# RWKV chunk inverse: the identity taken into each masked factor, the add replaced by a copy on ScalarE

## The chip, the cores and the metric

The kernel runs on one core of a Trainium2 chip. The metric is the device time of one execution in microseconds. Before the change it is 2451.85 us, the median of three runs (2451.59 to 2456.05).

## The reference

Two model blocks follow one another on a sequence of 256 tokens of width 1024, in fp32. The first block is a SwiGLU feed-forward layer, a mixing layer and a second feed-forward layer. The mixing layer has two parts side by side: dilated window attention, and a bidirectional RWKV-7 recurrence. The second block has two layers of windowed attention with an mLSTM, a dense feed-forward layer and a mixture of eight experts. The change touches the RWKV part alone. Per direction and head, the reference walks over the tokens with a 64 x 64 state:

```
def _rwkv7_step(state, inp):
    r, w, k, v, kk, kka = inp
    sa = jnp.einsum('dbhvk,dbhk->dbhv', state, kk)
    state = state * w[..., None, :] - sa[..., :, None] * kka[..., None, :] + v[..., :, None] * k[..., None, :]
    y = jnp.einsum('dbhvk,dbhk->dbhv', state, r)
    return state, y
```

There are 8 heads of 64 and 2 directions. The kernel doesn't walk token by token. It cuts the 256 tokens into four chunks of 64. Inside a chunk the removal terms (sa) depend on one another through a strictly triangular 64 x 64 matrix, so a chunk needs the inverse of "identity minus a strictly triangular matrix".

## The kernel before

`program` (L1634) runs the layers one after another. Each is written as a Python generator that yields now and then, and helpers such as `weave` run two of them in turn. `mix1` (L778) runs the RWKV part with `weave(self.rwkv(mp, me, R, yT), side, 4)`: after every fourth yield of `rwkv`, one step of `side` is emitted; what is left of `side` is emitted after it. `side` is `mod(0)` (L829). It streams 24 MB of modulation weights in 24 loads of 1 MB through three buffers, multiplies each load by a conditioning vector in four products of 512 columns (L837), and after every second load copies (L840), transposes (L843) and reduces (L845) the outcome. It has 36 steps.

The order of instructions on an engine isn't the order in which they are written. The framework's planner takes, engine by engine, what it believes to be ready, in the order of writing, by its own estimate of durations; each engine then runs its list in order, waiting on semaphores.

`rwkv` (L508) works on 8 groups: 4 pairs of heads (`ct`), each in 2 directions (`d`). `group(ct, d, sh)` (L539) prepares decays and scaled keys on ScalarE, VectorE and GpSimd (L569 to L608, the first products being L569 and L570), multiplies them (L623), and masks the outcome into `LM` (L626). A group holds four units `u`, each two chunks in two partition halves of 64 lanes (`halves`), so every small product below is 64 x 64 and the two halves use different parts of TensorE. After each direction pair comes `finish(ct)`. PSUM buffers have the tags c0, c1, c2, two buffers each; a group uses the tag of its number modulo 3.

The inverse is built by doubling the size of the blocks that are inverted (1 to 64 in six levels). `X` is the inverse so far, `Y` its transpose. Level 0 has no product: GpSimd masks `LM` (L654, once per half), VectorE adds the identity (L656) and transposes (L657). Each of the levels 1 to 5 has a product with `LM` into PSUM (L663, 8 small products), a mask on VectorE that reads PSUM (L665), a product with `Y` (L670, again 8), an add on VectorE that reads PSUM (L672), and a 32 x 32 block transpose on VectorE (L673); the last level adds into `Y` (L675) and has no transpose. A level ends with a yield. After the levels the inverse is multiplied with the right-hand sides (L680, 8 products of 128 columns), copied (L682, L684), and used to the end of the group (L715).

In fp32 each product is two TensorE instructions in the profile, so a line with 8 products shows 16.

Of the kernel before, what the change touches and what calls it, by code (L numbers as in the profile page):

```python
# [13 lines left out]
OP = mybir.AluOpType  # L14
# [8 lines left out]
FT = 22  # L23
# [10 lines left out]
class Builder:  # L34
# [473 lines left out]
    def rwkv(self, mp, me, R, yT):  # L508

        nc = self.nc  # L510
# [6 lines left out]
        lvl = self.load_const(mp, "k_lvl", nc.sync)  # L517
# [16 lines left out]
        def tmpt(name, bufs=1):  # L534
            return me.tile([128, S], F32, name=name, bufs=bufs)

        halves = [slice(0, 64), slice(64, 128)]

        def group(ct, d, sh):  # L539
            tag = "c%d" % ((2 * ct + d) % DEEP)  # L540
# [76 lines left out]
            LM = me.tile([128, 4, 4, 64], F32, name="LM", bufs=DEEP)  # L617
# [18 lines left out]
            if d == 1:  # L636
                s = tmpt("ksum")
# [5 lines left out]
            lv = self.psum(4, 64, tag=tag)  # L643
# [4 lines left out]
            nc.scalar.copy(RHS[:, :, 64:128], lv)  # L648
            square = lambda n, bufs=1: mp.tile([128, 4, 64], F32, name=n, tag=n + tag, bufs=bufs)
            over = lambda i: lvl[:, i][:, None, :].to_broadcast([128, 4, 64])  # L650
            X, Y = square("X"), square("Y")

            for c in range(2):
                nc.gpsimd.tensor_tensor(Y[halves[c]], LM[halves[c], :, 2 * c],  # L654
                                        lvl[halves[c], 0][:, None, :].to_broadcast([64, 4, 64]), op=OP.mult)
            nc.vector.tensor_tensor(Y, Y, over(6), op=OP.add)  # L656
            nc.vector.transpose(X, Y)  # L657
            for li in range(1, 6):
                fp = self.psum(4, 64, tag=tag)
                for u in range(4):  # L660
                    for c in range(2):
                        ps = halves[c]
                        nc.tensor.matmul(fp[ps, u], LM[ps, u, 2 * c], X[ps, u], start=True, stop=True)  # L663
                F = square("FT")
                nc.vector.tensor_tensor(F, fp, over(li), op=OP.mult)  # L665
                yp = self.psum(4, 64, tag=tag)
                l, r_ = (Y, F) if li < 5 else (F, Y)
                for u in range(4):
                    for ps in halves:
                        nc.tensor.matmul(yp[ps, u], l[ps, u], r_[ps, u], start=True, stop=True)  # L670
                if li < 5:
                    nc.vector.tensor_tensor(X, yp, X, op=OP.add)  # L672
                    nc.vector.transpose(Y, X)  # L673
                else:
                    nc.vector.tensor_tensor(Y, yp, Y, op=OP.add)  # L675
                yield
            pp = self.psum(4, 128, tag=tag)
            for u in range(4):
# [9 lines left out]
            for u in range(4):  # L688
                t, hh = divmod(u, 2)
# [5 lines left out]
            yp = self.psum(2, 2, 64, tag=tag)  # L695
            for u in range(4):
                t, hh = divmod(u, 2)
# [7 lines left out]
            for u in range(4):  # L705
                t, hh = divmod(u, 2)
# [66 lines left out]

        shs = [{} for _ in range(4)]
        g = [group(ct, d, shs[ct]) for ct in range(4) for d in range(2)]
        yield from chain(g[0], g[1], finish(0, shs[0]), g[2], g[3], finish(1, shs[1]), g[4], g[5], finish(2, shs[2]), g[6], g[7], finish(3, shs[3]))

# [806 lines left out]
def host_consts():  # L1584
    f = np.float32
    out = {"k_ident": np.eye(128, dtype=f)}
    i = np.arange(128)
    t, s = i[:, None], i[None, :]
    same = (t // 64) == (s // 64)
    lm = np.zeros((128, 2, 2, 2, 64), f)  # L1590
    lv = np.zeros((128, 7, 64), f)
    for d in range(2):
        before = (t < s) if d == 0 else (t > s)
        incl = before | (t == s)
        b, n = before[:64, :64], incl[:64, :64]
        for c in range(2):
            lm[c * 64:c * 64 + 64, d, c] = np.stack([-b.astype(f), -n.astype(f)], 1)
            lm[64 - c * 64:128 - c * 64, d, c] = np.stack([b, n], 1)
    for li, m in enumerate((1, 2, 4, 8, 16, 32)):
        lv[:, li] = np.tile(((t // (2 * m) == s // (2 * m)) & (t // m != s // m))[:64, :64], (2, 1))  # L1600
    lv[:, 6] = np.tile(np.eye(64), (2, 1))
    out["k_lm"] = lm
    out["k_lvl"] = lv
    out["k_blk"] = same.astype(f)
    q = np.arange(S)
    diff = np.abs(q[:, None] - q[None, :])
    cnt = (diff <= 64).astype(np.int64) + (diff % 4 == 0) + (diff % 16 == 0)
    bias = np.where(cnt > 0, np.log(np.maximum(cnt, 1).astype(np.float64)), -1e30).astype(f)
    out["k_mask1"] = np.ascontiguousarray(bias.reshape(2, 128, S).transpose(1, 0, 2))
    pos = np.arange(S, dtype=f)  # L1610
    inv = (f(10000.0) ** (-np.arange(0, 64, 2, dtype=f) / f(64))).astype(f)
    ang = (pos[:, None] * inv[None, :]).astype(f)
    c, sn = np.cos(ang).astype(f), np.sin(ang).astype(f)
    C = np.concatenate([c, c], 1)
    Sg = np.concatenate([-sn, sn], 1)
    tab = np.stack([C / 8, Sg / 8, C, Sg], 1).astype(f)
    t4 = np.arange(S)
    iq = (f(10000.0) ** (-np.arange(16, dtype=f) / f(16))).astype(f)
    ar = ((t4 // 64).astype(f)[:, None] * iq[None]).astype(f)
    ac = ((t4 % 64).astype(f)[:, None] * iq[None]).astype(f)  # L1620
    cr, sr, cc, sc = (np.cos(ar).astype(f), np.sin(ar).astype(f), np.cos(ac).astype(f), np.sin(ac).astype(f))
    C2 = np.concatenate([cr, cr, cc, cc], 1)
    S2 = np.concatenate([-sr, sr, -sc, sc], 1)
    tab2 = np.stack([C2 / 8, S2 / 8, C2, S2], 1).astype(f)
    out["k_rope2"] = np.ascontiguousarray(tab2.reshape(2, 128, 4, 64).transpose(1, 0, 2, 3))
    ok = np.stack([t <= s, t >= s], 1)
    out["k_tri"] = ok.astype(f)
    out["k_trib"] = np.where(ok, 0.0, -1e30).astype(f)
    out["k_iota"] = np.ascontiguousarray(np.broadcast_to(np.arange(1, 257, dtype=f).reshape(2, 128), (128, 2, 128)))
    out["k_rope1"] = np.ascontiguousarray(tab.reshape(2, 128, 4, 64).transpose(1, 0, 2, 3))  # L1630
    return out
# [32 lines left out]
def arrange(inputs):  # L1664
    out = {}
    for n in _RAW:
        a = np.asarray(inputs[n])
        if n not in _WHOLE:
            a = a.reshape(a.shape[1:])
        if n in ("rwkv_w2", "rwkv_a2"):  # L1670
            a = a.reshape(128, 512)
        if n == "w_router_2":
            a = a.reshape(KT, 128, 8).transpose(1, 0, 2)
        out[n] = np.ascontiguousarray(a)
    out["k_vec"] = pack_vec(vec_list(inputs))
    out.update(host_consts())
    return out
# [16 lines left out]
```

## Time and profile before

| what | value |
|---|---|
| median of three runs | 2451.85 us |
| the profiled execution | 2451.68 us |
| its span, first to last instruction | 2449.9 us |
| TensorE products busy | 2346.6 us (96%) |
| VectorE busy | 1614.4 us (66%) |
| ScalarE busy | 1307.0 us (53%) |
| GpSimd busy | 188.2 us (8%) |

The span is one execution on the chip. Busy times are sums over the whole span; the ends of TensorE products are modelled, so a busy TensorE isn't one at its peak. In the rows, PE is a TensorE product, PEld a weight load, DVE is VectorE, ACT is ScalarE, POOL is GpSimd, L665 is line 665 of the kernel. A form such as 64*64 64x128 f32 is the part of the array that is used (rows*columns) and the output (partitions x elements).

### The profile page before, as it was taken

To read this page: it belongs to the slowest core of one execution; us is meant where nothing else is said; L and a number is where in the kernel's file an instruction comes from. 1 tells how busy PE (TensorE), PEld (TensorE's weight loads), DVE (VectorE), ACT (ScalarE), POOL (GpSimd) and SP (SyncE) were. 2 spreads that over 40 slices of the span, in tenths; PEclk is the share of its full clock that TensorE was granted. 3 is DMA by queue.
4 is the path that set the end of the run, shared out by engine and by line. 5 is a ranking of instruction groups with operands and counts; after the bars stand their busy time and mean duration, and the time that the engine had idled before them with its cause. 6 is when DMAs were issued, how large, how long until landed. Compare 5 with 4: busy or idle time off the path is not lost. (4 is left out here: it accounts for less than half of the span.)

```text
span 2449.9 us, 38791 instructions
## 1 busy us (share of the span) xinstructions
PE 2346.6 (96%) x15592; PEld 1963.8 (80%) x15592; DVE 1614.4 (66%) x2427; ACT 1307.0 (53%) x2038; POOL 188.2 (8%) x248
## 2 busy tenths in 40 slices
PE   7998989979998999999999999989999999999996
PEld 7996866659998767799899886778888887788875
DVE  5555667656547466443333464669989989889897
ACT  5543644345545355433223243567887777777764
POOL 0001112110001000200100110020100110020000
PEclk9999999999999999999999999999999999999998
DMA  8654342275652350232322235469999999999993
GB/s 261 198 187 138 122 162 88 81 237 170 202 173 88 102 172 21 70 118 82 110 93 82 83 113 175 135 237 373 335 352 341 343 345 335 352 339 335 365 343 134
DMA packets 281100, 489.56 MB, mean 200 GB/s; under 512 B 11424, under 2 KB 116896, under 8 KB 280912
## 3 DMA queue, kind: packets, MB, share of 16 engines
q1 hardware_dynamic: 280832, 486.80, 58.2%
q8 instruction: 124, 2.03, 0.3%
q14 instruction: 64, 0.52, 0.1%
q0 software_dynamic: 80, 0.21, 0.0%
HBM read 485.92 MB, written 1.05 MB: 199 GB/s over the span
## 5 line engine op out<-in xcount | busy, mean ns | idle before, releaser
L150 DVE TENSOR_TENSOR wlo<-wraw,whi 128x1024 fp32r<-128x1024 f32 (+1 forms) x830 | 975.5, 1208 | 227.9 <-ACT whi L149 221.9
L149 ACT CAST whi<-wraw 128x1024 fp32r<-128x1024 f32 (+1 forms) x832 | 824.6, 1030 | 257.9 <-PE ps L162 102.2
L161 PE MATMUL gu<-xlo,whi 128*128 128x256 f32 x1408 | 394.4, 280 | 4.0 <-DVE xlo L193 2.4
L160 PE MATMUL gu<-xhi,whi 128*128 128x256 f32 x1408 | 394.6, 281 | 0.8 <-ACT xhi L200 0.8
L162 PE MATMUL gu<-xhi,wlo 128*128 128x256 f32 x1408 | 393.8, 280 | 0.0
L161 PE MATMUL gu<-wlo,X 128*128 128x512 f32 (+1 forms) x768 | 291.2, 379 | 4.4 <-DVE wlo L150 3.4
L162 PE MATMUL gu<-whi,X 128*128 128x512 f32 (+1 forms) x768 | 286.2, 373 | 0.0
L160 PE MATMUL gu<-whi,X 128*128 128x512 f32 (+1 forms) x768 | 285.1, 374 | 0.0
L161 PEld LDWEIGHTS gu<-xlo,whi 128*128 128x128 f32 x1408 | 264.8, 188 | 5.3 <-DVE xlo L193 2.9
L160 PEld LDWEIGHTS gu<-xhi,whi 128*128 128x128 f32 x1408 | 264.7, 188 | 2.2 <-ACT xhi L200 1.4
L162 PEld LDWEIGHTS gu<-xhi,wlo 128*128 128x128 f32 x1408 | 265.2, 188 | 0.0
L161 PEld LDWEIGHTS gu<-wlo,X 128*128 128x128 f32 x768 | 144.7, 188 | 45.5 <-DVE wlo L150 21.3
L160 PEld LDWEIGHTS gu<-whi,X 128*128 128x128 f32 x768 | 144.7, 188 | 25.5
L162 PEld LDWEIGHTS gu<-whi,X 128*128 128x128 f32 x768 | 144.7, 188 | 23.6
L274 DVE TENSOR_TENSOR hh<-sg,gu 128x256 f32<-128x256 f32 x88 | 36.8, 418 | 164.6 <-ACT sg L272 164.6
L161 PE MATMUL acc<-wlo,xhi 128*128 128x512 f32 (+1 forms) x368 | 141.8, 386 | 3.1 <-DVE wlo L150 3.1
L160 PE MATMUL acc<-whi,xhi 128*128 128x512 f32 (+1 forms) x368 | 140.8, 385 | 2.5 <-ACT whi L149 1.1
L162 PE MATMUL acc<-whi,xlo 128*128 128x512 f32 (+1 forms) x368 | 141.6, 385 | 0.1
L161 PE MATMUL dn<-wlo,hT 128*128 128x512 f32 x352 | 140.6, 399 | 0.0
L162 PE MATMUL dn<-whi,hT 128*128 128x512 f32 x352 | 138.6, 394 | 0.0
L160 PE MATMUL ps<-whi,hhi 128*128 128x512 f32 x352 | 137.2, 390 | 0.0
L162 PE MATMUL ps<-whi,hlo 128*128 128x512 f32 x352 | 137.1, 390 | 0.0
(461 smaller groups left out, 3740.7 us busy)
## 6 DMA issues: line engine op xcount, KB each, us to landing
wraw<-in_exp_w_dram SPq DMA_DIRECT2D x235, 1024.0 KB, 7.0
wraw<-in_w_mod_dram SPq DMA_DIRECT2D x48, 1024.0 KB, 5.2
wraw<-in_w_in_dram SPq DMA_DIRECT2D x29, 1024.0 KB, 5.2
wraw<-in_exp_w_dram SPq DMA_DIRECT2D x58, 512.0 KB, 6.7
wraw<-in_ffn_w_dram SPq DMA_DIRECT2D x28, 1024.0 KB, 5.3
wraw<-in_ffn_w_gate_dram SPq DMA_DIRECT2D x20, 1024.0 KB, 5.7
wraw<-in_ffn_w_up_dram SPq DMA_DIRECT2D x20, 1024.0 KB, 5.5
wraw<-in_ffn_w_down_dram SPq DMA_DIRECT2D x16, 1024.0 KB, 5.1
```

The lines of the kernel that those rows point to most:

```text
L149: nc.scalar.copy(hi, raw[:, k0:k0 + n])
L150: eng.tensor_tensor(lo, raw[:, k0:k0 + n], hi.bitcast(F32), op=OP.subtract)
L160: mm(out, l[0], r[0], start=start, stop=False)
L161: mm(out, l[0], r[1], start=False, stop=False)
L162: mm(out, l[1], r[0], start=False, stop=stop)
L274: nc.vector.tensor_tensor(hh, sg, pg[:, 1], op=OP.mult)
```

## The change

Level 0 now goes through the same loop as the others. In every level the product with `LM` is accumulated in PSUM onto an identity, which is put there by one more product per half: the 64 x 64 identity times four copies of itself, 256 columns. The masks now include the diagonal, so the masked factor is "identity plus masked product". The product with `Y` then gives the new `X` (or, in the last level, the new `Y`) without an add, and ScalarE copies it from PSUM. Level 0 multiplies `LM` by the identity and writes its masked product into `X`. `X` and `Y` become new tiles in each level, in the same one buffer each. The loop yields once a level, six times instead of five.

```diff
             X, Y = square("X"), square("Y")
-            for c in range(2):
-                nc.gpsimd.tensor_tensor(Y[halves[c]], LM[halves[c], :, 2 * c],
-                                        lvl[halves[c], 0][:, None, :].to_broadcast([64, 4, 64]), op=OP.mult)
-            nc.vector.tensor_tensor(Y, Y, over(6), op=OP.add)
-            nc.vector.transpose(X, Y)
-            for li in range(1, 6):
+            eye = lambda ps: lvl[ps, 6]
+            for li in range(6):
                 fp = self.psum(4, 64, tag=tag)
+                for ps in halves:
+                    nc.tensor.matmul(fp[ps], eye(ps), lvl[ps, 6][:, None, :].to_broadcast([64, 4, 64]), start=True, stop=False)
                 for u in range(4):
                     for c in range(2):
                         ps = halves[c]
-                        nc.tensor.matmul(fp[ps, u], LM[ps, u, 2 * c], X[ps, u], start=True, stop=True)
-                F = square("FT")
+                        nc.tensor.matmul(fp[ps, u], LM[ps, u, 2 * c], X[ps, u] if li else eye(ps), start=False, stop=u == 3)
+                F = square("FT") if li else X
                 nc.vector.tensor_tensor(F, fp, over(li), op=OP.mult)
-                yp = self.psum(4, 64, tag=tag)
-                l, r_ = (Y, F) if li < 5 else (F, Y)
-                for u in range(4):
-                    for ps in halves:
-                        nc.tensor.matmul(yp[ps, u], l[ps, u], r_[ps, u], start=True, stop=True)
-                if li < 5:
-                    nc.vector.tensor_tensor(X, yp, X, op=OP.add)
-                    nc.vector.transpose(Y, X)
-                else:
-                    nc.vector.tensor_tensor(Y, yp, Y, op=OP.add)
+                if li > 0:
+                    yp = self.psum(4, 64, tag=tag)
+                    l, r_ = (Y, F) if li < 5 else (F, Y)
+                    for u in range(4):
+                        for ps in halves:
+                            nc.tensor.matmul(yp[ps, u], l[ps, u], r_[ps, u], start=True, stop=True)
+                    if li == 5:
+                        Y = square("Y")
+                        nc.scalar.copy(Y, yp)
+                        yield
+                        break
+                    X = square("X")
+                    nc.scalar.copy(X, yp)
+                    Y = square("Y")
+                nc.vector.transpose(Y, X)
                 yield
...
-        lv[:, li] = np.tile(((t // (2 * m) == s // (2 * m)) & (t // m != s // m))[:64, :64], (2, 1))
+        lv[:, li] = np.tile((((t // (2 * m) == s // (2 * m)) & (t // m != s // m)) | (t == s))[:64, :64], (2, 1))
```

## Rows read from the trace of the kernel before

**Rows 1.** Busy by stretch: stretch, length, busy (instructions), clock, DMA, GB/s.
```profile
core 0: us, PE busy (x) PEld busy (x) DVE busy (x) ACT busy (x) POOL busy (x), PEclk, DMA share, GB/s
340.00:505.00 165.00, 156.95 (x2628) 107.38 (x2624) 112.84 (x308) 59.06 (x151) 28.66 (x38) 1.00 0.34 111
505.00:560.00 55.00, 40.96 (x243) 31.46 (x242) 32.77 (x47) 30.04 (x45) 11.53 (x14) 0.85 0.62 200
```

**Rows 2.** The same view in stretches of 20 us, one late in the stage.
```profile
480.00:500.00 20.00, 19.76 (x320) 11.49 (x316) 8.06 (x26) 3.57 (x10) 0.00 (x0) 1.00 0.70 226
```

**Rows 3.** Timeline, 400 to 406 us: start, duration, engine, line, operation, tiles, shape.
```profile
400.03 0.42 DVE L665 TENSOR_TENSOR FT<-c,k_lvl 128x256 f32<-128x256 f32 x1 [2.05 <-PE c L663]
400.35 0.70 PE L569 MATMUL c<-wd,wag 64*128 64x256 f32 x2
...
400.97 0.68 PE L670 MATMUL c<-FT,Y 64*64 64x64 f32 x16
401.58 0.70 PE L570 MATMUL c<-ad,wag 64*128 64x256 f32 x2
401.70 0.42 DVE L672 TENSOR_TENSOR X<-c,X 128x256 f32<-128x256 f32 x1 [0.66 <-PE c L670]
...
402.21 1.05 PE L837 MATMUL md<-wraw,cT 128*32 128x512 f32 x4
402.38 0.84 ACT L573 ACTIVATE sa<-c,hb 128x256 f32<-128x256 f32 x2 [1.63 <-PE c L570]
403.19 0.70 PE L569 MATMUL c<-wd,wag 64*128 64x256 f32 x2
...
403.82 0.68 PE L663 MATMUL c<-X,LM 64*64 64x64 f32 x16
...
404.43 0.70 PE L570 MATMUL c<-ad,wag 64*128 64x256 f32 x2
404.55 0.42 DVE L665 TENSOR_TENSOR FT<-c,k_lvl 128x256 f32<-128x256 f32 x1 [1.94 <-PE c L663]
...
405.06 1.04 PE L837 MATMUL md<-wraw,cT 128*32 128x512 f32 x2
...
406.03 0.68 PE L670 MATMUL c<-FT,Y 64*64 64x64 f32 x16
```

**Rows 4.** Timeline, one group's first level, 367 to 371 us.
```profile
367.02 0.68 DVE L626 TENSOR_TENSOR LM<-c,k_lm 128x512 f32<-128x512 f32 x1
...
367.78 1.52 POOL L654 TENSOR_TENSOR Y<-LM,k_lvl 64x256 f32<-64x256 f32 x2 [14.22 <-DVE LM L626]
...
369.33 0.42 DVE L656 TENSOR_TENSOR Y<-Y,k_lvl 128x256 f32<-128x256 f32 x1 [0.62 <-POOL Y L654]
...
369.79 0.45 DVE L657 STREAM_TRANSPOSE X<-Y 128x256 f32<-128x256 f32 x1
...
370.38 0.83 PE L663 MATMUL c<-X,LM 64*64 64x64 f32 x17 [0.25 <-DVE X L657]
```

**Rows 5.** Timeline, 128-column products of the inverse, and the block behind them.
```profile
373.89 1.09 PE L680 MATMUL c<-RHS,Y 64*64 64x128 f32 x16
...
374.81 0.62 PE L663 MATMUL c<-X,LM 64*64 64x64 f32 x14
```

**Rows 6.** By line: instruction, count, duration ns least/median/most, first and last start.
```profile
L665 DVE TENSOR_TENSOR FT<-c,k_lvl x40: 382/420/426, 344.2 to 496.8; 128x256 f32<-128x256 f32 x40
...
L672 DVE TENSOR_TENSOR X<-c,X x32: 385/416/425, 345.5 to 495.2; 128x256 f32<-128x256 f32 x32
...
L682 ACT COPY PQ<-c x8: 353/372/372, 361.0 to 501.2; 128x256 f32<-128x256 f32 x8
```

**Rows 7.** L837: its busy time alone by stretch (PE, PEld); a whole load, timeline.
```profile
340.00:505.00 165.00, 33.89 (x140) 4.61 (x135) 1.00 0.34 111
...
413.98 1.06 PE L837 MATMUL md<-wraw,cT 128*32 128x512 f32 x8
```

**Rows 8.** By line: a VectorE subtraction of the group's preparation, columns as in rows 6.
```profile
L584 DVE TENSOR_TENSOR E<-cs x8: 410/520/952, 331.0 to 455.6; 128x256 f32<-128x256 f32 x8
```

## The prediction

> **What bounds the kernel now.** I read the page first. Its engine line and its slices show TensorE busy nearly everywhere, but a busy TensorE in this trace includes modelled matmul ends, and the chain that ended last is only the closing 5 us, so neither says what bounds the stage that is changed. I went on to the table by stretch. The changed code runs from about 340 to 505 us: TensorE 156.95 busy of 165.00, VectorE 112.84, ScalarE 59.06, GpSimd 28.66, all at granted clock 1.00 [rows 1]. VectorE is idle for 52 us of it, ScalarE for 106, TensorE for 8.05. Late in the stage it is more lopsided: from 480 to 500 us TensorE 19.76 of 20, VectorE 8.06 [rows 2].
>
> Is TensorE full or only standing in a dependent chain? The timeline answers it [rows 3]. Follow one level of the inverse. The masked product on VectorE (L665) ends at 400.03 + 0.42 = 400.45; the product that needs it (L670) starts at 400.97. The add (L672) ends at 402.12; the next product that needs it (L663) starts at 403.82, 1.7 us later. The next L665 ends at 404.97; its L670 starts at 406.03. In between TensorE isn't idle: L569, L570 and L837 of other groups and of the side work stand in front, start behind start. Inputs are ready and wait for TensorE's queue. So here the TensorE queue sets the pace; VectorE and ScalarE wait for it.
>
> **The change, part by part.** Durations are from the profiled execution (2451.68 us; span 2449.9); the median of the runs, 2451.85, is 0.2 us off, so one base serves.
>
> (a) Identity products. Six levels in each of 8 groups (4 head pairs, 2 directions) get a product per 64-partition half with 256 moving columns: 48 pairs. The trace has no such pair. The nearest row is L680: 8 products of 64*64 with 128 columns, the halves alternating, so 1024 columns; from its start at 373.89 to the next block at 374.81 it holds the queue 0.92 us [rows 5]. A pair is 512 columns of the same tile: 0.46 us. Low end: an L670 block, 8 products of 64 columns, holds the queue from 400.97 to 401.58, 0.61 us [rows 3]; the 512 columns by which L680 exceeds it cost 0.92 - 0.61 = 0.31. High end: the two halves do not run side by side; then each costs what L569 does, a 256-column product on 64 partitions, 400.35 to 400.97, 0.62 us, a pair 1.24. A pair can start as soon as its PSUM buffer is free, which is when L665 has read it, so it stands behind L670 and beside the copy: off the dependent chain, but in the full queue. I take 0.46, since L680 has the same tile and alternates halves as the pair does: 48 x 0.46 = 22.1 us (14.9 to 59.5). It waits for nothing that L670 didn't wait for.
>
> (b) First level. Out: two GpSimd products, an add and a position in the chain for the transpose. In: 8 products (0.61 as any L670 block) and one masked product on VectorE. Latency before: L626 ends at 367.70, the transpose at 370.24, 2.54 us, and L663 starts at 370.38 [rows 4]. After: 0.61 plus the drain to VectorE and 0.42, about 1.2, with the transpose behind it beside L663. The chain gets 1.3 us shorter per group, 10.7 in all if the chain set the end; where the queue does, it buys only a place in the queue. TensorE gets 8 x 0.61 = 4.9 us. GpSimd loses 8 x 1.5, which held up nobody but this chain and a few VectorE operations: an L584, a plain VectorE subtraction, takes 0.41 at best and 0.95 at worst [rows 8]. If one operation a group is slowed so by these products, 8 x 0.54 = 4.3 us come back to VectorE; I value it at 0 on the path, since VectorE has 52 us to spare.
>
> (c) Add becomes copy. 32 adds of 0.416 us and 8 of the last level leave VectorE [rows 6], about 16.6 us; the mask of the first level and the add that it replaces cancel. 40 copies of 0.37 (L682, the same shape from PSUM) go to ScalarE, 59 + 15 = 74 us of 165: covered. The transpose now waits for a copy on another engine; behind it in VectorE's queue stand other groups' operations, and these have VectorE's spare 52 us. The copy is 0.05 us shorter than the add, 40 x 0.05 = 2 at best; if it is queued behind a longer ScalarE operation (the two L573, 0.84 [rows 3]) it is as much later. I take 0, with 2 less and 8 more as ends (one such delay of 0.2 us a copy).
>
> (d) Order. Each group has one more yield, so a quarter more of a side step per group: 25 of the 36 side steps stand inside the RWKV stage where 23 did. Nothing is added; two steps, at 1.06 us a load of four products [rows 7], move ahead: 0, at most 2 us either way. The mask tables change values only: 0.
>
> (e) What absorbs it. TensorE's 8.05 idle us in the stretch [rows 1] can take at most that; I take half, 4, because the eye products aren't ready wherever it idles.
>
> Sum: 22.1 + 4.9 - 4.0 = 23.0 us on the TensorE queue, 2451.7 + 23 = 2474.7, rounded to 2475. With the low price of the pair and all idle time used: 14.9 + 4.9 - 8.05 = 11.8, less 2 for (c) and 2 for (d): 2460. After the stage nothing takes this back: 505 to 560 us has TensorE busy 40.96 of 55 [rows 1], waiting for the results of this stage.
>
> **The rivals.**
> Faster: VectorE's evacuation of PSUM is what holds the levels, and the queue is full only because lower work is let in while the chain waits. For it: L837 products start in the very gaps in which L665 and L672 run [rows 3], and a level takes 5.06 us here (L670 at 400.97 and at 406.03) for two blocks of 0.61 and two VectorE operations of 0.42 on the path. Then the 16.6 us that leave VectorE are the gain and the identity products hide under the copy: 2451.7 - 16.6 = 2435. Against it: the 0.5, 1.7 and 1.06 us by which ready inputs wait for TensorE, and 52 us of idle VectorE. It decides as soon as the planner has fewer fillers than gaps.
> The Trainium skill, TensorEngine Tiling (Array Packing), "PSUM Bottleneck", says the same as a rule: array tiling speeds up the products but not the evacuation of PSUM, which may become the limit, and ScalarE and VectorE should share it. The change is that rule followed; this trace doesn't bear it out for this stage, since the evacuating engines are the ones with idle time.
>
> No change: the side work packs better. A load's four products take 1.06 us when they run together (x8) [rows 7], about as long as one of them alone (x2, 405.06 to 406.03, 0.97) [rows 3]; the stage spends 33.89 us on 140 instructions, 17.5 loads [rows 7], where 17.5 x 1.06 = 18.6 would do. If the identity products take the small gaps, whole loads move to one place: -15.3, and all idle time used, -8: 27.0 - 23.3 = +3.7, 2455. For it: the waste is there. Against: the same planner fills the other gap of each level, under L665, as before.
>
> Much slower: the halves run one after the other. 48 x 1.24 + 4.9 - 4 = 60.4: 2512. For it: each 256-column product is two instructions in a row on one half, and L569 shows 0.62 for that. Against: the L680 row, where consecutive products on different halves overlap.
>
> **How the numbers follow.** Forecast 0.62, own range 2460 to 2495 (the upper end: 0.46 raised to 0.75 a pair, plus 8 of (c)); no change 0.15; faster 0.16; much slower 0.07. A measurement of this kernel can tell about 0.2%, 4.9 us, from no change. The faster rival and a little of the second lie below 2446.8: 0.18; most of the second and the low edge of the first lie within: 0.12; the rest 0.70. Eight in ten: from 2444, which keeps the second rival and the near part of the first, to 2498, which leaves out the last.
>
> **What would show it.** Right: in the stretch of the RWKV levels the profile has some 190 new TensorE instructions with 256 columns (48 pairs, two instructions to a product), in the queue a pair holding about 0.46 us; the last L715 and the following stage come some 23 us later; VectorE's busy time there falls by 16 and its idle time rises; TensorE's idle time falls below 8. L670 still starts well after its L665 ends. Wrong: if L663 to L663 of one group gets shorter, or the L837 sum falls by more than 10 us, one of the first two rivals holds; if pairs hold the queue over 1 us, the third. If the stage after begins earlier than before, the reading of a full queue was wrong altogether.

## The result and the profile after

The changed kernel takes 2484.4 us (median of 4 runs, 2482.16 to 2486.8); the kernel before, beside it, 2452.4. The ratio is 1.0129, 95% interval 1.0117 to 1.0142: slower by 32.0 us, where 23 were forecast and 2444 to 2498 was the range. The profiled execution of the changed kernel is the longest of the four, 2486.8 us, 35.1 above the profiled one before. One of the ten executions of e9 below took 3690.2 us and is left out of its median.

The table by stretch of the changed kernel (columns as in [rows 1]):

```profile
340.00:505.00 165.00, 158.00 (x2446) 104.01 (x2448) 92.82 (x241) 64.74 (x170) 17.68 (x24) 0.97 0.24 77
```

TensorE is as busy as before, and VectorE (92.82 us after 112.84) has 20 us less to do in the same 165 us; yet the stage isn't over at 505 us. The number in brackets counts instructions: TensorE has 2446 in the stretch where [rows 1] had 2628, so fewer of the stage's products were done by then. The closing copy of the eight groups shows where the stage ends, before (L715) and after (L718); the columns are count, duration, first and last start:

```profile
L715 ACT COPY PZ<-c x8: 265/312/372, 364.9 to 506.0; 128x256 f32<-128x256 f32 x4, 128x128 f32<-128x128 f32 x4
```
```profile
L718 ACT COPY PZ<-c x8: 266/320/373, 364.7 to 544.9; 128x256 f32<-128x256 f32 x4, 128x128 f32<-128x128 f32 x4
```

The first group ends at the same time, the last one 38.9 us later. The next stage's first product (L160 into the buffer of the side work) starts at 512.23 before and at 547.63 after, 35.4 us later, and nothing behind it gives that back (the two profiled executions end 35.1 us apart):

```profile
512.23 0.73 PE L160 MATMUL md<-whi,xhi 128*128 128x512 f32 x2 [0.29 <-ACT whi L149]
```
```profile
547.63 0.48 PE L160 MATMUL md<-whi,xhi 128*128 128x512 f32 x1
```

The timeline of the changed kernel in one level, the answer to [rows 3]; L669 is the product with Y, L657 the identity pair, L676 the copy, L661 the product with LM, L663 the mask:

```profile
416.92 0.68 PE L669 MATMUL c<-FT,Y 64*64 64x64 f32 x16
417.43 0.60 PE L657 MATMUL c<-k_lvl 64*64 64x256 f32 x4
417.64 0.37 ACT L676 COPY X<-c 128x256 f32<-128x256 f32 x1 [0.95 <-PE c L669]
417.96 0.70 PE L570 MATMUL c<-ad,wag 64*128 64x256 f32 x2
...
418.59 0.68 PE L661 MATMUL c<-X,LM 64*64 64x64 f32 x16
...
419.20 1.05 PE L840 MATMUL md<-wraw,cT 128*32 128x512 f32 x2
419.31 0.42 DVE L663 TENSOR_TENSOR FT<-c,k_lvl 128x256 f32<-128x256 f32 x1 [0.82 <-PE c L661]
...
420.17 0.68 PE L669 MATMUL c<-FT,Y 64*64 64x64 f32 x16
```

The pair starts where the dependent chain would let TensorE go: beside the copy. But the queue doesn't stand still there. The pair holds it from 417.43 to 417.96, 0.53 us, and only then comes L570, the next group's preparation. Some of it comes back: in front of the pair, L669 holds the queue 0.51 us (416.92 to 417.43), where L670 in front of L570 held it 0.61 in [rows 3]; at this place a pair adds 0.43. The chain's own product L661 finds its input ready at 418.01 and starts at 418.59. All pairs are there (count, duration in ns, first and last start):

```profile
L657 PE MATMUL c<-k_lvl x192: 376/377/631, 342.1 to 533.1; 64*64 64x256 f32 x192
```

192 instructions are 48 pairs. If each TensorE instruction is charged with the time from its start to the next one's start, from 300 us to the first L160, this sum grows by 35.3 us: the identity pairs take 26.4, the first level's products 5.1, and the products of the side work 2.9 more than before; all the rest together is 1.0. Beside the pairs, the product with LM takes 1.2 more in the five old levels, the product with Y 2.0 less.

### The profile page after: what moved, and what is told of

It reads as the page before. It is cut to its first block, busy times and chain, and to the rows that moved or that the text cites. A ratio compares the mean times of both kernels' runs of the same rounds, so it can differ in the third digit from the quotient of the medians.

```text
span 2485.0 us, 39432 instructions
## 1 busy us (share of the span) xinstructions
PE 2382.7 (96%) x15912; PEld 1980.9 (80%) x15912; DVE 1604.0 (65%) x2387; ACT 1320.5 (53%) x2078; POOL 175.0 (7%) x232
## 5 line engine op out<-in xcount | busy, mean ns | idle before, releaser
L160 PE MATMUL gu<-xhi,whi 128*128 128x256 f32 x1408 | 395.1, 281 | 1.2 <-ACT xhi L200 0.8
L160 PE MATMUL gu<-whi,X 128*128 128x512 f32 (+1 forms) x768 | 285.0, 374 | 0.0
L160 PEld LDWEIGHTS gu<-xhi,whi 128*128 128x128 f32 x1408 | 265.0, 188 | 2.4 <-ACT xhi L200 1.4
L161 PEld LDWEIGHTS gu<-wlo,X 128*128 128x128 f32 x768 | 144.7, 188 | 45.5 <-DVE wlo L150 21.2
L160 PEld LDWEIGHTS gu<-whi,X 128*128 128x128 f32 x768 | 144.8, 188 | 25.5
L160 PE MATMUL acc<-whi,xhi 128*128 128x512 f32 (+1 forms) x368 | 141.3, 386 | 2.4 <-ACT whi L149 1.1
L274 DVE TENSOR_TENSOR hh<-sg,gu 128x256 f32<-128x256 f32 x88 | 36.8, 418 | 164.6 <-ACT sg L272 164.6
L160 PE MATMUL ps<-whi,hhi 128*128 128x512 f32 x352 | 137.2, 390 | 0.0
```

Of the source, the lines that this page charges most:

```text
L160: mm(out, l[0], r[0], start=start, stop=False)
L161: mm(out, l[0], r[1], start=False, stop=False)
L274: nc.vector.tensor_tensor(hh, sg, pg[:, 1], op=OP.mult)
```

## The experiments

All medians are beside the kernel before on the same chip: 2451.6 us beside e1 to e8, 2452.2 beside e9 and e10, 2453.6 beside e11 and e12. A difference between runs of different sets holds up to 2 us of that.

| run | median us | ratio, 95% interval |
|---|---|---|
| e1 no identity products | 2449.3 | 0.9989, 0.9979 to 0.9998 |
| e2 before, identity pairs added | 2472.6 | 1.0086, 1.0069 to 1.0103 |
| e3 identity in bf16 | 2457.0 | 1.0023, 1.0013 to 1.0032 |
| e4 before, one more yield | 2445.2 | 0.9971, 0.9959 to 0.9982 |
| e5 changed, one yield less | 2489.8 | 1.0146, 1.0126 to 1.0167 |
| e6 signed diagonal, X first | 2447.7 | 0.9983, 0.9974 to 0.9993 |
| e7 changed, add on VectorE | 2477.9 | 1.0106, 1.0089 to 1.0123 |
| e8 bf16 identity, whole array | 2457.7 | 1.0027, 1.0018 to 1.0037 |
| e9 signed diagonal | 2446.0 | 0.9976, 0.9966 to 0.9986 |
| e10 e4, first level on VectorE | 2443.6 | 0.9966, 0.9952 to 0.9979 |
| e11 changed, first level as before | 2478.8 | 1.0106, 1.0089 to 1.0123 |
| e12 e4, first level in the loop | 2453.6 | 1.0000, 0.9990 to 1.0009 |

**e1.** The changed kernel without its identity products.
```diff
-                for ps in halves:
-                    nc.tensor.matmul(fp[ps], eye(ps), ..., start=True, stop=False)
-                        nc.tensor.matmul(fp[ps, u], LM[...], X[ps, u] if li else eye(ps), start=False, stop=u == 3)
+                        nc.tensor.matmul(fp[ps, u], LM[...], X[ps, u] if li else eye(ps), start=True, stop=True)
```


> The changed kernel (2484.4 us) without the identity products: the level is product, mask, product, copy, first level in the loop, all else kept; the inverse it computes is therefore not the inverse. Theory Q (TensorE's queue is full in this stage, the 48 identity pairs pay 0.53 us each, 25.4 us): 2484.4 - 25 = 2459, so 5 to 8 us above the kernel before (2452), for the eight first-level products. Rival C (the copies on ScalarE and the order that follows from them lengthen the levels, the identity products stand beside them): 2475 to 2485. Rival V (VectorE's work holds the levels): below 2445.

2449.3: the whole loss goes with the identity products, though the copies, the first level in the loop and the masks stay. It is 10 us below Q's 2459, and in neither rival's range: without the 48 pairs the kernel is 35.1 us faster, 0.73 each, where 0.53 is what a pair holds of the queue. More on that stands behind the experiments. Its busy times in the stage:

```profile
340.00:505.00 165.00, 161.10 (x2766) 112.33 (x2763) 98.06 (x267) 72.25 (x193) 16.80 (x22) 0.99 0.35 114
```

TensorE gets through 2766 instructions there, VectorE works 15 us less than in [rows 1], and the end is where it was. VectorE's relief bought nothing that shows, against rival V.

**e2.** The kernel before, with identity pairs in five levels.
```diff
                 fp = self.psum(4, 64, tag=tag)
+                for ps in halves:
+                    nc.tensor.matmul(fp[ps], lvl[ps, 6], lvl[ps, 6][:, None, :].to_broadcast([64, 4, 64]), start=True, stop=False)
```


> The kernel before, with the 40 identity pairs of levels 1 to 5 added in front of the masked product's products; the old masks drop the diagonal, so only TensorE work is added. Theory Q: 40 x 0.53 = 21 us more, 2473, between 2467 and 2480. Rival C: within 5 us of 2452, since the add stays on VectorE. Rival V: no change.

21.0 us more for 40 pairs, 0.53 each, as Q said: the price of the pair in the queue, paid in full. The row that counts them:

```profile
L661 PE MATMUL c<-k_lvl x160: 375/377/428, 344.0 to 509.5; 64*64 64x256 f32 x160
```

**e3, e8.** The identity in bf16; in e8 one product over the whole array for both halves. The cut is e8's.
```diff
-                for ps in halves:
-                    nc.tensor.matmul(fp[ps], eye(ps), lvl[ps, 6]..., start=True, stop=False)
+                nc.tensor.matmul(fp, idb, eyeb[:, None, :].to_broadcast([128, 4, 64]), start=True, stop=False)
```


> The changed kernel with the identity products in bf16 (0 and 1 are exact), one instruction a product instead of two, nothing else changed but one small cast at the start. Theory Q: a pair falls from 0.53 to at most half of it in the queue, so at least 48 x 0.26 = 13 us less, 2460 to 2472. Rival C: 2480 to 2486.

> The changed kernel with one bf16 identity product a level over the whole array, for both halves at once, in place of four fp32 instructions. Theory Q with the price set by the moving columns: one instruction of 256 columns, at most 0.2 us in the queue with its block change, 48 x 0.2 = 10 us above e1: 2453 to 2460, about as the bf16 halves (2457). Rival (what costs is the number of instructions and the block changes): a change of array shape before and after it makes it dearer than the halves, 2460 to 2470.

```profile
L659 PE MATMUL c<-eyeb x96: 267/269/293, 339.7 to 499.4; 64*64 64x256 bf16 x96
```

The row is e3's. Both fall by some 27 us to 7.6 and 8.4 us above e1, so a level's identity costs 0.16 and 0.18 us. e3 lies below its range for Q (2460 to 2472), which took the fall of 13 us as the least; e8 is in its own. The time follows the TensorE work of the same identity; e8 needs half the instructions of e3 and gains nothing by it.

**e4, e5.** One yield a group, added to the kernel before or taken from the changed one. The cut is e4's.
```diff
             nc.vector.transpose(X, Y)
+            yield
             for li in range(1, 6):
```


> The kernel before with one more yield a group, so that 25 instead of 23 of the 36 side steps are emitted inside the RWKV stage, as in the changed kernel; no instruction is added. Theory Q: within 3 us of 2452. Rival S (the side work's place in the order makes the loss): 10 us or more above 2452.

> The changed kernel without the yield of the first level, so that 23 side steps stand inside the RWKV stage as in the kernel before; no instruction is added or removed. Order and clock theory (of the changed kernel's loss 10 us are not instructions but the order that came out, with the granted clock at half for 10 us at 392 us): another order moves the time by 3 to 10 us, and if the clock stays at 1.00 in the stage it is 2472 to 2480. Rival (the identity products simply cost 0.73 us each here): 2482 to 2492.

e4's expectation for Q failed: the yield is worth 6.4 us in the kernel before, with no instruction added. Two side steps earlier in the order matter. Where they do, the trace shows: the last closing copy (L716 there) starts only 1.1 us earlier, at 504.9, but the next stage's first product 7.0 us earlier:

```profile
505.21 0.47 PE L160 MATMUL md<-whi,xhi 128*128 128x512 f32 x1
```

The kernel before still has 16 instructions of L837 behind that copy, two loads, and L160 starts behind the side work's last product; e4 has none there.

In the changed kernel it isn't shown that the yield is worth anything. The median of e5 is 5.4 us longer, but it lies in the ranges of both its theories, and its four runs differ in their mean granted clock: three at 0.981 and 0.982 took 2489.4 to 2492.4 us, the one at 0.985 took 2482.3, no longer than the changed kernel's two at 0.985 and 0.986 (2482.7 and 2482.2). In e5's trace too the clock was at half for 10 us in the stage, so it does not tell the clock's part either.

**e7.** The adds are back on VectorE, the identity pairs kept.
```diff
-                    X = square("X")
-                    nc.scalar.copy(X, yp)
-                    Y = square("Y")
+                    nc.vector.tensor_tensor(X, yp, X, op=OP.add)
```


> The changed kernel with the adds of the kernel before back on VectorE in place of the copies (masks of levels 1 to 5 without the diagonal, so the 48 identity pairs are kept as pure TensorE work). Theory Q: the same TensorE queue, 2470 to 2490, whatever VectorE does with 17 us more. Rival V: the adds return and it is 10 us or more above 2484. Order theory: it differs from 2484 by up to 10 us either way.

2477.9, within what Q gives: with 17 us more on VectorE (estimated from its adds) it is 6.5 us faster than the changed kernel, not slower. Part of these 6.5 is the clock. In the changed kernel the granted clock falls to its lower level (1.2 GHz) at 391.9 us for 10.2 us; here it stays at 1.00:

```profile
380.00:400.00 20.00, 18.64 (x314) 12.59 (x314) 16.22 (x47) 6.08 (x14) 3.44 (x5) 1.00 0.01 3
```
```profile
380.00:400.00 20.00, 17.90 (x237) 12.01 (x235) 12.45 (x36) 6.59 (x17) 3.44 (x5) 0.80 0.16 54
```

(The first is e7, the second the changed kernel.) How long TensorE stood before the fall, and how long a pair takes in it, by the changed kernel's timeline:

```profile
391.56 0.44 PE L768 MATMUL c<-k_ident,yn 128*128 128x128 f32 x2 [1.78 <-DVE yn L763]
...
396.50 1.06 PE L657 MATMUL c<-k_lvl 64*64 64x256 f32 x4
```

It stood 1.78 us behind the closing steps of the first head pair. A pair takes 1.06 us in the fall and 0.60 at 417.43. At half clock 10.2 us do the work of 5.1, so the fall costs at most 5.1 us. The runs agree: two of the changed kernel's four have a mean clock of 0.983 and took 2486.1 and 2486.8 (the profiled one), the two at 0.985 and 0.986 took 2482.7 and 2482.2. That is 4 us in two runs of four, 2 in the median. e7's runs, 2477.5 to 2479.7, lie 2.5 us or more below the shorter two as well, so the clock isn't all of it.

**e6, e9.** The same level without any identity product. Within a block that is already inverted, the product with LM gives the inverse minus the identity; if minus the identity is put into LM, it gives minus the identity there, and a mask with -1 on the diagonal turns it into the identity.
```diff
+                nc.vector.tensor_tensor(LM[ps, :, 2 * c], LM[ps, :, 2 * c], ...lvl[ps, 6]..., op=OP.subtract)
+                nc.vector.tensor_tensor(Y[ps], LM[ps, :, 2 * c], ...lvl[ps, 0]..., op=OP.mult)
+            nc.vector.transpose(X, Y)
...
-        lv[:, li] = ... & (t // m != s // m)) | (t == s))
+        lv[:, li] = ... & (t // m != s // m)).astype(f) - (t == s))
```


> The change's level without identity products: minus the identity is put into LM once a group (two small VectorE operations), and the level masks carry -1 on the diagonal, so the masked product comes out with the identity in it; the first level is a mask of LM on VectorE, two operations of 64 partitions; the copies stay on ScalarE. Theory Q (TensorE's queue sets the pace): the 48 pairs and the eight first-level products are gone, e1's 2449 less 8 x 0.61 = 2444, between 2438 and 2450. Rival C (the copy on ScalarE lengthens the level): above 2452.

e6 wrote X in place of Y in the first level, and so built another matrix than the inverse; its time is that of the same instructions.

> The change's level (product, mask, product, copy on ScalarE) with the identity at no cost on TensorE: minus the identity goes into LM once a group, the level masks carry -1 on the diagonal, and the first level is a mask on VectorE; the outcome is the kernel's. It differs from e6 only in which of X and Y the first level writes first, as in the kernel before. Theory Q: 2444 to 2450, below the kernel before (2452) and 35 us below the changed kernel. Rival C (the copy on ScalarE lengthens the level): above 2452.

2446.0, ratio 0.9976, as Q said: faster than both kernels, and within 1 us of e4, which has the yield alone. Its stage again has busy copies on ScalarE (73.94 us against 59.06) and the same end:

```profile
340.00:505.00 165.00, 160.68 (x2698) 110.30 (x2700) 107.61 (x296) 73.94 (x196) 16.73 (x23) 0.99 0.35 116
```

**e10.** The kernel of e4, with the first level's masks on VectorE.
```diff
-                nc.gpsimd.tensor_tensor(Y[halves[c]], LM[halves[c], :, 2 * c],
+                nc.vector.tensor_tensor(Y[halves[c]], LM[halves[c], :, 2 * c],
```


> The kernel before with the extra yield of e4 (2445.2) and the first level's two masked products on VectorE in place of GpSimd: the way from LM to the first product gets some 0.7 us shorter in each of 8 groups, and TensorE's work stays as it is. Theory Q (the latency of the first level buys nothing while TensorE's queue is full): within 3 us of 2445. Rival L (the chain of a group sets the pace): 8 x 0.7 = 6 us less, 2439 or below.

2443.6, 1.6 us below e4, as Q said: a shorter first level off TensorE buys next to nothing. It is the lowest median of the study (0.9966), but its interval and e4's overlap.

**e11, e12.** The first level alone, taken out of the change or put into the kernel of e4. The cut is e11's; in both, the first level's mask is set to fit.
```diff
-            for li in range(6):
+            for c in range(2):
+                nc.gpsimd.tensor_tensor(Y[halves[c]], LM[halves[c], :, 2 * c], ..., op=OP.mult)
+            nc.vector.tensor_tensor(Y, Y, over(6), op=OP.add)
+            nc.vector.transpose(X, Y)
+            yield
+            for li in range(1, 6):
```


> The changed kernel with the first level as it was before (two masked products on GpSimd, an add and a transpose on VectorE, then a yield), and the identity pairs, masks and copies of levels 1 to 5 as changed. Theory Q (the queue's sum): 8 x (0.53 + 0.61) = 9 us less than 2484, 2470 to 2478. Theory Q2 (in the changed trace the first level also takes some 7 us from the end of L626 to the mask, because its products stand in the queue, where GpSimd took 2.5; that thins the overlap of the groups): more than 12 us less, 2466 to 2472. Rival L (the first level in the loop was the gain of the change): 2490 or more.

> The kernel before with the yield of e4 (2445.2) and only the first level changed: 8 identity pairs and 8 products on TensorE and one mask with the diagonal, in place of the GpSimd products and the add; the levels 1 to 5 as before. Theory Q: 8 x (0.53 + 0.61) = 9 us above e4, 2451 to 2457. Theory Q2: 12 us or more above e4, 2457 or more. Rival L: below 2445.

e12 is 8.4 us above e4, as Q said (9), or 6.4 if each is taken from the kernel before in its own set. e11 is 5.6 us below the changed kernel (6.8 so taken), less than Q's 9, just above Q's range, and much less than Q2's 12. The first level in the loop is a cost of 6 to 8 us, not a gain.

## Why the prediction was right

The mechanism held: TensorE's queue is full in this stage, and products added off the dependent chain are paid in full. Step by step:

- (a) was taken at 0.46 us a pair. In the trace it holds the queue 0.53, of which about 0.1 comes back in the block in front of it; e2 says 0.53 in the end: 48 x 0.53 = 25.4 instead of 22.1. The two halves do run side by side; the much slower rival is out.
- (b): the sum was right. First-level products and their 8 pairs were 4.9 + 3.7 = 8.6; e12 says 6.4 to 8.4. The forecast latency of 1.2 us was wrong. In one group of the changed kernel L626 ends at 403.45 and the first mask starts at 410.70, 7.25 us against 2.54 to the transpose's end in [rows 4]; its products stand in the full queue:

```profile
402.76 0.69 DVE L626 TENSOR_TENSOR LM<-c,k_lm 128x512 f32<-128x512 f32 x1 [0.34 <-PE c L623]
...
410.70 0.42 DVE L663 TENSOR_TENSOR X<-c,k_lvl 128x256 f32<-128x256 f32 x1 [2.27 <-PE c L661]
```

- (c) was 0 and is about 0 by itself: e1 is 4.1 us above e4, where the first-level products explain 4.9, and e9, with the copies and no pairs, is within 1 us of e4. Beside the fp32 pairs the version with the add is 6.5 us faster (e7), the clock included.
- (d) was 0, at most 2 either way. In the kernel before it is 6.4 us gained (e4), so the size was wrong there; in the changed kernel it is open (e5).
- (e) was wrong: I let idle time absorb 4 us. e2 shows the pairs paid whole, 21.0 of 21.2, and from 340 us to the first L160 TensorE is idle 8.4 us before and 8.5 after. Nothing was absorbed.
- A clock fall inside the stage, up to 5.1 us in the profiled run and 2 in the median, was not in the sum at all.
- The upper end of my own range, 0.75 us a pair and 8 us of (c), adds up to 2497, not 2495.

So the forecast was 9 us low: 3.3 by (a), 4 by (e) and about 2 by the clock, all in one direction. With the measured parts the sum is 25.4 + 4.9 + 2.0 = 32.3 for 32.0, if the yield is worth nothing here, as e5's one run at the same clock says. If it is worth 6.4 as in the kernel before, 6 us stay open, and that 23 came as near as it did was then partly luck, since (d) hid them. One run doesn't decide it.

What moves with the order can be read in the traces, though no run varied it alone. A block of the side work's products (an uninterrupted row of them) holds the queue about 1 us, whether it has two instructions (405.06 to 406.03 in [rows 3]) or eight (413.98 in [rows 7], to the next block here):

```profile
414.98 1.09 PE L680 MATMUL c<-RHS,Y 64*64 64x128 f32 x16
```

All versions have the same 192 instructions there, but in different numbers of blocks, counted in the traces:

| version | blocks | us in the queue, idle time left out, clock falls included |
|---|---|---|
| before | 38 | 40.5 |
| e4 | 35 | 36.8 |
| changed | 40 | 41.8 |
| e1 | 35 | 36.7 |
| e7 | 35 | 37.4 |
| e11 | 42 | 44.0 |

That is 3.7 of the 6.4 us that e4 gains, 4.4 of the 6.5 by which e7 is faster than the changed kernel, 5.1 of the 9.7 that e1 gained beyond the price of the pairs (some 2 more are the changed kernel's clock, the rest stays open), and 2.2 that e11 lost of its 9. What makes the planner split the loads more or less isn't shown.

One of my signs of being wrong came: L663 to L663 of one group got shorter. Read at the masks behind it, from the second to the fourth of the fourth group, it takes 8.87 us before (from 400.03, [rows 3]) and 6.97 after:

```profile
408.90 0.41 DVE L665 TENSOR_TENSOR FT<-c,k_lvl 128x256 f32<-128x256 f32 x1
```
```profile
415.99 0.42 DVE L663 TENSOR_TENSOR FT<-c,k_lvl 128x256 f32<-128x256 f32 x1 [0.30 <-PE c L661]
...
422.96 0.41 DVE L663 TENSOR_TENSOR FT<-c,k_lvl 128x256 f32<-128x256 f32 x1
```

Over the eight groups the mean from the first level's outcome to the last level's fell from about 22.4 to 19.4 us, and still the stage got longer, because the next group begins later: the groups, which overlapped or followed within 4 us, now stand up to 12 us apart. Neither of the two faster rivals follows from it (e1, e9); the sign was ill chosen, since how long a level takes depends on what else the queue takes in between.

The faster rival is refuted: with VectorE relieved and the identity free or absent (e1, e9) the time is at most some 6 us below before, no more than the yield alone gives. The rule of the Trainium skill that the prediction cites (TensorEngine Tiling (Array Packing), "PSUM Bottleneck": use both ScalarE and VectorE for the evacuation) brings nothing in this stage: the evacuations that e9 leaves on ScalarE gain nothing over e4, and e7, with them back on VectorE, is faster than the changed kernel. The rival of better packing didn't come in the change either: in 340 to 505 us the side work's products take 24.22 us for 98 instructions, 0.247 each, where [rows 7] had 0.242, and they stand in 40 blocks for 38.

## What to carry to other kernels

Before adding work to an engine "in the shadow of a wait", look whether that engine waits at all: if inputs stand ready before it takes them, every added instruction costs its full time in the queue. Read that time from the start of the nearest row of the same tile to the start of the next block, not from its busy time or the chain's latency. And look for the arithmetic that gives the same term for nothing: a diagonal in an operand that is loaded anyway replaced 48 pairs of products. Where a planner orders the instructions, leave room in the range for what another order does: here 6.4 us for a yield.

## What the runs showed of the hardware

- The granted clock fell to half inside the stage in the changed kernel (391.9 us, for 10.2 us), in e5 (395.0, 10.2) and late in e11 (490.1, 3.4). In the first two it came behind a wait of TensorE of 1.78 us; the kernel before waits 1.62 us at the same place, from 389.4 to 391.0, and keeps 1.00 through the levels. What tips it wasn't tried.
- A bf16 identity of 256 columns over the whole array (one instruction, 0.18 us a level) costs as much as two over the halves (0.16), so the number of instructions doesn't set the price. That 256 columns are paid once in both fits this; no run varied the columns.
- A block of the side work's products (128*32, 512 columns, four to a load) holds TensorE's queue about 1 us with two instructions or with eight.
- Moving two side steps forward in the order, with no instruction changed, is worth 6.4 us in the kernel before (e4); taking the adds off VectorE beside the same yield (e9) adds nothing to it.
